# Cross-covariance attention: Q and K of a third of the heads in 8 KB rows

## The chip, the cores and the metric

The kernel runs on one core of a Trainium2 chip. A core has a matrix engine (TensorE, PE in the profile), three engines for elementwise work (VectorE or DVE, ScalarE or ACT, GpSimd or POOL), and SyncE (SP), which here issues all transfers between HBM and on-chip memory. Sixteen DMA engines move the bytes of each transfer side by side. Every engine works through its own instructions in order and waits for the others on semaphores. Matrix results go to PSUM, which GpSimd does not use here; everything else lies in SBUF, with 128 partitions.

The metric is the device time of one execution, in microseconds (us), as the median of several runs.

## The reference

There are 8 x 12 = 96 heads, with 512 positions n and 64 columns d each, all in float32. Attention is between columns, not positions:

```python
Q_norm = Q / (np.linalg.norm(Q, axis=-2, keepdims=True) + 1e-10)
K_norm = K / (np.linalg.norm(K, axis=-2, keepdims=True) + 1e-10)
attn = np.einsum('bhnd,bhne->bhde', Q_norm, K_norm)        # 64 x 64 per head
attn = np.exp(attn - np.max(attn, axis=-1, keepdims=True))
attn = attn / (np.sum(attn, axis=-1, keepdims=True) + 1e-10)
return np.einsum('bhnd,bhde->bhne', V, attn)
```

A norm is taken over the positions, so each head needs 64 norms of q, 64 of k and one 64 x 64 product (its gram). Q, K, V and the output are 12 MiB each: 36 MiB come in and 12 MiB go out.

## The kernel before

**Tiles.** A unit u is four heads (24 units), a pair s two units (12 pairs), a double pair w four units (6 of them, each with 1 MiB pieces of V).

**Loads.** `load_qk` (lines 170 to 180) brings Q and K of a pair as [128 partitions, 2 units, 16 positions, 64]. Each partition holds 16 neighbouring positions of one head, 4 KB of it, so 32 partitions (a row group of TensorE) hold one head. The last unit comes in 2 KB rows. `load_v` brings V with 32 positions to a partition, in 8 KB rows. There are three buffers for pairs of Q and K and three for V. Stores (`store`) write 512 KB in 2 KB rows from 13 buffers `so`.

**Grams.** `cast_qk` (line 196) casts a unit's Q and K on VectorE into one bf16 tile `qkb` with q and k side by side (two buffers). `grams` (208) multiplies each head's [q|k] with itself, 16 steps x 4 heads of 128 x 128 in four row groups. The result holds qq, qk, kq and kk. `squares` (222) picks the diagonals of qq and kk on VectorE (two instructions per pair, 64 partitions x 512), `sums` (237) reduces them to squared norms, `cross` (232) copies kq out of PSUM, `powers` (242) makes the reciprocal norms with a logarithm and an exponential on ScalarE.

**Attention.** `scale_k` (248) scales k's side on GpSimd or VectorE. `logits` transposes, `exps` scales by q's norm and exponentiates, `normalise` (271) divides and writes the bf16 tile `ab`. V is cast to bf16 (`cast_v`, on GpSimd or, late in the kernel, VectorE), transposed on TensorE (`vtrans`), copied out (`vcopy`) and multiplied with `ab` (`outs`); `ocopy` brings the result to `so`.

**Order.** All of this is written as pieces (`piece(key, engines, after, behind, rank, ...)`) with a guessed cost for each engine that may do it. `Order.run` plays them through and gives every engine a fixed order; nothing moves at run time. Keys: `cq` casts, `gr` grams, `sq` squares, `kq` cross, `rd` sums, `pw` powers, `sc` scale of k, `rq` scales of q, `lg` logits, `ex` exponentials, `nm` normalise, `cv` cast of v, `vt` transposes, `vc` their copies, `ou` outputs, `oc` their copies, `st` stores. From pair `BOTH` on, copies and casts may also go to VectorE (line 394, 409 ff., 430). All DMAs stand in one queue of SyncE in the planned order: a load that waits for a free buffer holds all loads and stores behind it.

Of the kernel before, what the change touches and what calls it, by code (L numbers as in the profile page):

```python
# [8 lines left out]
F32 = mybir.dt.float32  # L9
BF16 = mybir.dt.bfloat16  # L10
AF = mybir.ActivationFunctionType
# [91 lines left out]
def kernel(  # L103
# [13 lines left out]
    TAIL = 2  # L117
    WIDE = U - 1
    ONE = 3
    BOTH = S - 8  # L120
# [7 lines left out]
    Vu = V.rearrange("b h (p t) d -> (b h p) (t d)", t=2 * T).rearrange("(w r p) x -> w r p x", r=2, p=128)  # L128
# [9 lines left out]
    NB = dict(qk=3, v=3, vb=2, qkb=2, vt=2, so=13, sm=2, ab=4)  # L138
# [4 lines left out]
    qkp = ctx.enter_context(tc.tile_pool(name="qkp", bufs=NB["qkb"]))  # L143
    vtp = ctx.enter_context(tc.tile_pool(name="vtp", bufs=NB["vt"]))
# [5 lines left out]
    grams_only = ExitStack()  # L150
# [8 lines left out]

    qk32, v32, vb, qkb, gram, scr, kq, n2, r8, kqs, rq, lg, ex, ab, vps, vt, po, so = ({} for _ in range(18))  # L160
# [9 lines left out]
    def load_qk(s, x, r):  # L170

        w, e = divmod(s, 2)
        if s not in qk32:
            qk32[s] = qp.tile([128, 2, 2, T, D], F32, name="qk32")
        if 2 * s + (r or 0) >= WIDE:
            nc.sync.dma_start(out=qk32[s][:, x, r].rearrange("p (m j) d -> p m (j d)", m=2), in_=(Qw, Kw)[x][U - 1])
        elif r is None:
            nc.sync.dma_start(out=qk32[s][:, x].rearrange("p r t d -> p r (t d)"), in_=(Qu, Ku)[x][w, e])
        else:
            nc.sync.dma_start(out=qk32[s][:, x, r].rearrange("p t d -> p (t d)"), in_=(Qu, Ku)[x][w, e, :, r])  # L180
# [20 lines left out]

    def cast_v(eng, w, r, c):

        if w not in vb:
            vb[w] = vbp.tile([128, 2 * T, 2, D], BF16, name="vb")
        copy(eng, vb[w][:, c * T:(c + 1) * T, r], v32[w, r][:, c].rearrange("p (t d) -> p t d", d=D))

    def grams(u):


        s, r = divmod(u, 2)
        if r == 0:
            gram[s] = ps_g.tile([128, HU, 2, 2, 2 * D], F32, name="gram")
        for t in range(T if u < WIDE else J):
            for h in range(HU):
                if u < WIDE:
                    x = qkb[u][32 * h:32 * (h + 1), t, :]
                else:
                    x = qkb[u][64 * (h % 2):64 * (h % 2 + 1), J * (h // 2) + t, :]
                nc.tensor.matmul(gram[s][:, h, r, 0], x, x, start=(t == 0), stop=(t == (T if u < WIDE else J) - 1))  # L220

    def squares(s, n):

        if n == 0:
            scr[s] = small.tile([128, 2 * HU, D], F32, name="scr")
        half = (LO, HI)[n]
        nc.vector.scalar_tensor_tensor(  # L227
            out=scr[s][half], in0=gram[s][half, :, :, 0, half].rearrange("p h r d -> p (h r) d"), scalar=1e-20,
            in1=eye2[half, None, :].to_broadcast([D, 2 * HU, D]), op0=ALU.add, op1=ALU.mult,
        )  # L230

    def cross(eng, s):

        kq[s] = small.tile([128, 2 * HU, D], F32, name="kq")
        copy(eng, kq[s][HI], gram[s][HI, :, :, 0, LO].rearrange("p h r d -> p (h r) d"))

    def sums(s):
        n2[s] = small.tile([128, 2 * HU], F32, name="n2")
        nc.vector.tensor_reduce(out=n2[s], in_=scr[s], axis=mybir.AxisListType.X, op=ALU.add)  # L239

    def powers(s):

        ln = small.tile([128, 2 * HU], F32, name="ln")
        r8[s] = small.tile([128, 2 * HU], F32, name="r8")
# [3 lines left out]
    def scale_k(eng, s):  # L248
        kqs[s] = small.tile([128, 2 * HU, D], F32, name="kqs")
# [4 lines left out]
    def scales_q(s):  # L254

        rq[s] = small.tile([128, HU], F32, name="rq")
# [67 lines left out]

    abs_ = []
# [5 lines left out]
    def size(key):  # L331
        if key[0] == "gr" and key[1] >= WIDE:
            return 64
        return 8 if key[0] == "vt" and key[-1] is not None else {"gr": 128, "lg": 8, "vt": 16, "ou": 16}[key[0]]
# [3 lines left out]
    R = dict(cq=2.5, gr=2.471, sq=0.756, kq=1, rd=3.457, pw=3.5, sc=1, rq=1.9, lg=5, ex=1.1, nm=2.545, cv=1.165, vt=0.9, vc=1.1, ou=2, oc=0.9)  # L338
    BIAS = dict(sc=-0.6, kq=5, cv=1, vc=-0.3, oc=0.6)
    QK_PACE, V_FROM, V_PACE, ST_LAG = 0.631, 0.0377, 0.7486, 1.5133  # L340
# [4 lines left out]
    def piece(key, engines, after, behind, rank, fn, *args):  # L345
        if key[0] in ("cv", "vc", "oc", "kq", "sc"):
# [8 lines left out]
    def parts(s):  # L355
        return (0, 1) if s < ONE or s == S - 1 else (None,)

    def loaded(x, s, r):
        return ("l" + "qk"[x], s, r if len(parts(s)) == 2 else None)

    last = None
    for s in range(S):
        free = [back("cq", 2 * s + r, 2 * NB["qk"], x) for r in range(2) for x in range(2)]
        for r in parts(s):
            at = QK_PACE * (2 * s + (r or 0)) / U
            for x in range(2):
                key = loaded(x, s, r)
                piece(key, {"DMA": X if r is not None else 2 * X}, free, [last], at, load_qk, s, x, r)
                last = key
    for u in range(U):  # L370
        s, r = divmod(u, 2)
        piece(("cq", u, 0), {"DVE": 0.72}, [loaded(0, s, r), back("gr", u, NB["qkb"])], [back("cq", u, 1, 1)], R["cq"] + 0.01 * u, cast_qk, u, 0)
        piece(("cq", u, 1), {"DVE": 0.72}, [loaded(1, s, r)], [("cq", u, 0)], R["cq"] + 0.01 * u, cast_qk, u, 1)
        piece(("gr", u), {"PE": 1.6}, [("cq", u, 0), ("cq", u, 1), back("kq", s, 1)], [back("gr", u, 1)], R["gr"] + 0.01 * u, grams, u)
    for s in range(S):
        SM = NB["sm"]

        piece(("sq", s, 0), {"DVE": 0.70}, [("gr", 2 * s), ("gr", 2 * s + 1), back("rd", s, SM)], [], R["sq"] + 0.01 * s, squares, s, 0)
        piece(("sq", s, 1), {"DVE": 0.70}, [("gr", 2 * s), ("gr", 2 * s + 1)], [("sq", s, 0)], R["sq"] + 0.01 * s, squares, s, 1)
        piece(("kq", s), {"ACT": 0.60, "DVE": (0.70, BIAS["kq"])}, [("sq", s, 0), ("sq", s, 1), back("sc", s, SM)], [], R["kq"] + 0.01 * s, cross, s)  # L380
        piece(("rd", s), {"DVE": 0.69}, [("sq", s, 0), ("sq", s, 1), back("pw", s, SM)], [], R["rd"] + 0.01 * s, sums, s)
        piece(("pw", s), {"ACT": 0.5}, [("rd", s), back("rq", s, SM), back("sc", s, SM)], [], R["pw"] + 0.01 * s, powers, s)
        piece(("sc", s), {"POOL": (1.04, BIAS["sc"]), "DVE": 1.2}, [("pw", s), ("kq", s), back("lg", s, SM)], [], R["sc"] + 0.01 * s, scale_k, s)
        piece(("rq", s), {"ACT": 0.45}, [("pw", s), back("ex", s, SM)], [], R["rq"] + 0.01 * s, scales_q, s)
        piece(("lg", s), {"PE": 0.6}, [("sc", s), back("ex", s, 1)], [], R["lg"] + 0.01 * s, logits, s)
        piece(("ex", s), {"ACT": 1.30}, [("lg", s), ("rq", s), back("nm", s, NB["sm"])], [], R["ex"] + 0.01 * s, exps, s)
# [84 lines left out]
```

## Time and profile before

| | before |
|---|---|
| median of three runs | 130.85 us (130.26 to 130.95) |
| the profiled execution | 130.86 us |
| its span, first to last instruction | 129.1 us |
| last instruction of VectorE ends | 114.1 us |
| last copy to `so` ends (ScalarE) | 117.4 us |
| last store issued / landed | 119.3 / 128.1 us |
| bytes moved, mean rate | 50.64 MB, 392 GB/s |
| VectorE casts of Q and K (L200) | 48, mean 799 ns |
| VectorE squares (L227) | 24, mean 688 ns |
| GpSimd casts of V (L168) | 19, mean 1162 ns |
| GpSimd scale of k (L250) | 12, mean 1179 ns |

The profile is one execution. A group of its page gives the count, the busy time in us and the mean in ns. The slices cut the span into 40 parts of 3.2 us and give the busy share in tenths. The "landing" of a DMA is when its semaphore is complete.

### The profile page before, as it was taken

What the parts mean: (1) busy time and instruction counts of PE and PEld (TensorE: products, weight loads), DVE (VectorE), ACT (ScalarE), POOL (GpSimd) and SP (SyncE); (2) the same over time, 40 slices, a digit from 0 to 9 for tenths busy, and PEclk for the clock granted to TensorE, in tenths of its full rate; (3) what the DMA queues carried; (4) which work ended last, traced back from release to release, by engine and by line L of the source; (5) the groups of instructions that cost most, each with busy time, mean ns of one, the idle gap of its engine ahead of it and who ended that gap; (6) DMA issues with size and microseconds to landing.
All of it is one profiled execution on the core that took longest, in us unless ns stands there. A gap on an engine that the chain in (4) does not pass through costs nothing.

```text
span 129.1 us, 4881 instructions
## 1 busy us (share of the span) xinstructions
PE 77.8 (60%) x2128; PEld 63.3 (49%) x2128; DVE 91.0 (71%) x140; ACT 72.5 (56%) x220; POOL 37.3 (29%) x39
## 2 busy tenths in 40 slices
PE   0154384994837648967682986697785858382000
PEld 0144372773636537856572865486664746271000
DVE  3444649849999389699986798997999799830000
ACT  3000441569777085497783798383947969973000
POOL 3005406300813914043058003223463270300000
PEclk9999999999975685599999599655799999955555
DMA  4999999999999999999999999999999999999982
GB/s 133 389 430 410 432 399 409 408 416 409 422 406 411 404 408 410 402 413 430 410 414 406 416 415 418 405 420 415 405 410 403 405 399 406 402 407 406 408 312 75
DMA packets 15605, 50.64 MB, mean 392 GB/s; under 512 B 1120, under 2 KB 1632, under 8 KB 14176
## 3 DMA queue, kind: packets, MB, share of 16 engines
q1 hardware_dynamic: 15584, 50.34, 98.0%
q8 instruction: 16, 0.26, 0.8%
q14 instruction: 5, 0.04, 0.1%
HBM read 37.75 MB, written 12.58 MB: 390 GB/s over the span
## 4 chain that ended last, share of the span: by engine, by line
DMA 50%; DVE 16%; PE 10%; ACT 8%; issue 3%; SPq 1%; POOL 1%; ACTq 0%; POOLq 0%; DVEq 0%
DMA qk<-in_K_dram 21%; DMA v<-in_V_dram 15%; DMA qk<-in_Q_dram 14%; DVE qkb L200 7%; PE gram L220 6%; ACT so L164 3%; DVE scr L227 3%; DVE vt L166 2%; PE po L306 2%; DVE ab L278 2%; PE vps L289 2%; ACT ex L269 2%; ACT vt L164 2%; DVE n L239 1%; SPq L180 1%
## 5 line engine op out<-in xcount | busy, mean ns | idle before, releaser
L220 PE MATMUL gram<-qkb 32*128 32x128 bf16 (+1 forms) x1504 | 36.6, 259 | 21.7 <-DVE qkb L200 15.4
L200 DVE CAST qkb<-qk 128x1024 bf16<-128x1024 f32 x48 | 37.4, 799 | 11.7 <-DMA qk<-in_Q_dram 5.2
L220 PEld LDWEIGHTS <-qkb 32*128 32x128 bf16 (+1 forms) x1504 | 30.5, 116 | 26.8 <-DVE qkb L200 18.1
L168 POOL TENSOR_SCALAR vb<-v 128x1024 bf16<-128x1024 f32 x19 | 21.9, 1162 | 46.7 <-DMA v<-in_V_dram 46.4
L164 ACT COPY so<-po 128x512 f32<-128x512 f32 x45 | 25.0, 592 | 7.6 <-PE po L306 7.5
L164 ACT COPY vt<-vps 128x1024 bf16<-128x1024 bf16 (+1 forms) x18 | 17.8, 987 | 16.9 <-PE vps L289 16.8
L306 PE MATMUL po<-ab,vt 128*64 128x128 bf16 x384 | 21.3, 260 | 6.7 <-issue 2.8
L250 POOL TENSOR_TENSOR kqs<-kq,r 64x512 f32<-64x512 f32 x12 | 14.2, 1179 | 26.1 <-ACT r L246 14.1
L306 PEld LDWEIGHTS <-vt 128*64 128x64 bf16 x384 | 15.5, 131 | 10.8 <-issue 5.8
L289 PE MATMUL vps<-identb,vb 128*128 128x128 bf16 x192 | 16.7, 236 | 6.6 <-POOL vb L168 3.9
L227 DVE SCALAR_TENSOR_TENSOR scr<-gram,eye 64x512 f32<-64x512 f32 x24 | 16.5, 688 | 5.6 <-PE gram L220 5.3
L289 PEld LDWEIGHTS <-vb 128*128 128x128 bf16 x192 | 12.6, 105 | 9.6 <-POOL vb L168 4.9
L269 ACT ACTIVATE ex<-lg,rq 128x64 f32<-128x64 f32 x48 | 14.5, 322 | 2.8 <-PE lg L263 2.8
L164 ACT COPY kq<-gram 64x512 f32<-64x512 f32 x12 | 7.0, 581 | 14.4 <-DVE scr L227 14.0
L278 DVE TENSOR_TENSOR ab<-ex,rinv 64x256 bf16<-64x256 f32 x24 | 13.5, 560 | 0.6
L269 ACT ACTIVATION_READ_ACCUMULATOR ex<-lg,rq 128x1 f32 x48 | 10.2, 213 | 0.0
L263 PE MATMUL lg<-eye,kqs 64*128 64x64 f32 x48 | 6.6, 266 | 4.1 <-POOL kqs L250 2.8
L239 DVE TENSOR_REDUCE n<-scr 128x8 f32<-128x512 f32 x12 | 8.1, 678 | 0.1
L166 DVE COPY vt<-vps 128x1024 bf16<-128x1024 bf16 (+1 forms) x8 | 7.9, 1019 | 0.1
L263 PEld LDWEIGHTS lg<-eye,kqs 64*128 64x128 f32 x48 | 4.7, 162 | 6.0 <-POOL kqs L250 3.6
L166 DVE CAST vb<-v 128x1024 bf16<-128x1024 f32 x5 | 5.1, 1012 | 0.9 <-DMA v<-in_V_dram 0.9
L275 DVE RECIPROCAL rinv<-esum 128x4 f32<-128x4 f32 x12 | 2.1, 171 | 2.5 <-ACT ex L269 2.5
(15 smaller groups left out, 15.8 us busy)
## 6 DMA issues: line engine op xcount, KB each, us to landing
out_dram<-so SPq DMA_DIRECT2D x23, 512.0 KB, 10.2
v<-in_V_dram SPq DMA_DIRECT2D x11, 1024.0 KB, 17.9
qk<-in_Q_dram SPq DMA_DIRECT2D x8, 1024.0 KB, 18.2
qk<-in_K_dram SPq DMA_DIRECT2D x8, 1024.0 KB, 18.8
qk<-in_Q_dram SPq DMA_DIRECT2D x8, 512.0 KB, 12.1
qk<-in_K_dram SPq DMA_DIRECT2D x8, 512.0 KB, 12.5
v<-in_V_dram SPq DMA_DIRECT2D x2, 512.0 KB, 10.7
out_dram<-so SPq DMA_DIRECT2D x2, 256.0 KB, 9.1
```

Source lines behind the costliest of these rows:

```text
L164: nc.scalar.copy(o, i)
L166: nc.vector.tensor_copy(o, i)
L168: nc.gpsimd.tensor_scalar(out=o, in0=i, scalar1=1.0, scalar2=0.0, op0=ALU.mult, op1=ALU.add)
L200: nc.vector.tensor_copy(qkb[u][:, :, x * D:(x + 1) * D], qk32[s][:, x, r])
L220: nc.tensor.matmul(gram[s][:, h, r, 0], x, x, start=(t == 0), stop=(t == (T if u < WIDE else J) - 1))
L227: nc.vector.scalar_tensor_tensor(out=scr[s][half], in0=gram[s][half, :, :, 0, half].rearrange("p h r d -> p (h r) d"), scalar=1e-20, in1=e ...
L250: (nc.vector if eng == "DVE" else nc.gpsimd).tensor_tensor(out=kqs[s][HI], in0=kq[s][HI], in1=r8[s][HI, :, None].to_broadcast([D, 2 * HU, ...
L263: nc.tensor.transpose(l[:, h, :], kqs[s][HI, 2 * h:2 * h + 2].rearrange("p r d -> p (r d)"), eye2[HI])
L269: nc.scalar.activation(e[:, h, :], lg[s][:, h, :], AF.Exp, scale=rq[s][:, h:h + 1], accum_out=z[:, h:h + 1])
L278: nc.vector.tensor_tensor(out=a[half, :, half], in0=e[half], in1=ri[half, :, None].to_broadcast([D, HU, D]), op=ALU.mult,)
L289: nc.tensor.transpose(ps[:, c, n, :], vb[w][:, J * c + j].rearrange("p r d -> p (r d)"), identb)
L306: nc.tensor.matmul(po[s, x][e * D:(e + 1) * D, j].rearrange("p r d -> p (r d)"), v, ab[s][:, h, :])
```

## The change

For the double pairs w = 2 and 3 (pairs m = 4 to 7, 32 heads), Q and K come like V: 32 positions of a head in one partition, 8 KB rows, 1 MiB per transfer. Then 16 partitions hold a head, and a row group of 32 partitions holds two heads. To keep them apart, VectorE makes two copies of q in bf16, each with the other head's partitions multiplied by zero (`mask_q`), and the gram multiplies [q|k] of the row group with both masked q (64 matmuls of 128 columns per unit, as before). The result has qq and kq for both heads but no kk. k's squared norms are made another way: squares on ScalarE in f32 (`square_k`), halved five times by additions on GpSimd or VectorE (`fold_k`), and a matmul with a 0/1 matrix that adds each head's 16 partitions into a spare corner of the gram's PSUM (`norms_k`). Squares, copy, sums, powers and scaling are then done once for a double pair of 16 heads with 64 x 1024 elements, where two pairs had 64 x 512 (`big_squares` and so on). A double group holds the four banks of PSUM until `kQ`, `sQ` and `lK` are done; the next grams wait for these.

Four constants are added, `vb` gets a third buffer and `so` has 11 instead of 13, outputs may go to VectorE from pair 5 on (`BOTH`, 4 before), the last double pair is transposed in whole pieces, and the planner's ranks and paces are new, so the order of nearly all instructions is another. Bytes moved are the same, and so are the other 64 heads' steps.

```diff
-    TAIL = 2
+    TAIL = 4
...
-    BOTH = S - 8
+    BIG = (2, 3)
+    BOTH = S - 7
...
-    NB = dict(qk=3, v=3, vb=2, qkb=2, vt=2, so=13, sm=2, ab=4)
+    NB = dict(qk=3, v=3, vb=3, qkb=2, vt=2, so=11, sm=2, ab=4)
...
+        if big(m):
+            nc.sync.dma_start(out=qk32[m][:, x].rearrange("p c t d -> p (c t d)"), in_=(Qb, Kb)[x][w, e])
...
+    def mask_q(u):
+        mqb[u] = mqp.tile([128, T, 2, D], BF16, name="mqb")
+        for a in range(2):
+            nc.vector.tensor_scalar(
+                out=mqb[u][:, :, a], in0=qkb[u][:, :, :D], scalar1=half_of[:, a:a + 1], scalar2=None, op0=ALU.mult)
+
+    def square_k(u):
+        m, c = divmod(u, 2)
+        if c == 0:
+            ksq[m] = ksp.tile([128, 2, T, D], F32, name="ksq")
+        nc.scalar.activation(ksq[m][:, c], qk32[m][:, 1, c], AF.Square)
+
+    def fold_k(eng, m, part):
+        e = nc.vector if eng == "DVE" else nc.gpsimd
+        if part == 0:
+            e.tensor_tensor(out=ksq[m][:, 0], in0=ksq[m][:, 0], in1=ksq[m][:, 1], op=ALU.add)
+            return
+        ksum[m] = small.tile([128, D], F32, name="ksum")
+        n = T // 2
+        while n:
+            o = ksq[m][:, 0, :n] if n > 1 else ksum[m][:, None, :]
+            e.tensor_tensor(out=o, in0=ksq[m][:, 0, :n], in1=ksq[m][:, 0, n:2 * n], op=ALU.add)
+            n //= 2
...
+    def norms_k(m):
+        w, r = divmod(m, 2)
+        o = gram_of(w)[HI, 0, 4 * D:4 * D + 16].rearrange("p (h r) -> p h r", r=2)
+        nc.tensor.matmul(o[:, :, r], ksum[m], head_of, start=True, stop=True)
+
+    def big_grams(u):
+        m, c = divmod(u, 2)
+        w, r = divmod(m, 2)
+        g = gram_of(w)
+        for t in range(T):
+            for n in range(HU):
+                rows = slice(32 * n, 32 * (n + 1))
+                o = g[:, n, :4 * D].rearrange("p (a r d) -> p a r d", a=2, r=2)[:, :, r]
+                nc.tensor.matmul(o, qkb[u][rows, t], mqb[u][rows, t], start=(c == 0 and t == 0), stop=(c == 1 and t == T - 1))
...
+        if m >= NB["qk"] and big(m - NB["qk"]):
+            free += [("ks", 2 * (m - NB["qk"]) + i) for i in range(2)]
...
+        if big(m) and u % 4 == 0 or not big(m) and i == 0:
+            wait, release = release, [("kQ", w), ("sQ", w), ("lK", w)] if big(m) else [("kq", m)]
...
+            piece(("mq", u), {"DVE": 0.66}, [("cq", u, 0), back("gr", u, NB["qkb"])], [], R["mq"] + 0.01 * u, mask_q, u)
...
+            piece(("ks", u), {"ACT": 1.15}, [loaded(1, m, i)] + free, [back("ks", u, 1)] if i else [], R["ks"] + 0.01 * u, square_k, u)
...
+                    piece(("ka", m, n), {"POOL": 2.15, "DVE": (1.15, BIAS["ka"])}, [("ka", m, 0)] + [("kn", x) for x in older[:len(older) - 1]] if n else [("ks", u - 1), ("ks", u)], [],
+                          R["ka"] + 0.02 * m, fold_k, m, n)
+
+                piece(("kn", m), {"PE": 0.3}, [("ka", m, 1)], [("gr", 4 * w + 3)], R["kn"] + 0.02 * m, norms_k, m)
...
+        piece(("sQ", w), {"DVE": 1.2}, [("gr", 4 * w + k) for k in range(4)] + before(g, "rd", "sc"), [], R["sq"] + n, big_squares, w)
+        piece(("kQ", w), {"ACT": 1.15, "DVE": (1.2, BIAS["kq"])}, [("sQ", w)], [], R["kq"] + n, big_cross, w)
+        piece(("rD", w), {"DVE": 1.2}, [("sQ", w)] + before(g, "pw"), [], R["rd"] + n, big_sums, w)
...
+        piece(("lK", w), {"ACT": 0.25}, [("kn", 2 * w), ("kn", 2 * w + 1)] + free, [], R["lk"] + n, logs_k, w)
+        piece(("pW", w), {"ACT": 0.5}, [("rD", w), ("lK", w)] + before(g, "rq", "sc"), [], R["pw"] + n, big_powers, w)
+        piece(("sC", w), {"POOL": (2.1, BIAS["sc"]), "DVE": 1.25}, [("pW", w), ("kQ", w)] + before(g, "lg"), [], R["sc"] + n, big_scale_k, w)
+        piece(("rQ", w), {"ACT": 0.45}, [("pW", w)] + before(g, "ex"), [], R["rq"] + n, big_scales_q, w)
```

What the order becomes: VectorE gets 16 masks, two of the four first folds, both scalings of k, 12 output copies (3 before), 4 casts of v (5) and 4 copies of vt (5 and 3 half ones). GpSimd gets two first folds and all four fold tails, 20 casts of v (19) and 8 scalings of k (12). ScalarE gets 8 squares, 36 output copies (45) and 20 copies of vt (17 and a half one). SyncE issues as many transfers as before; 21 stores instead of 20 stand behind the last load of V.

## The prediction

> **What bounds the kernel now.** I read the page's busy shares and slices first, then the DMA rows, then the engines by stage, then single groups.
>
> ```profile
> PE 77.8 (60%) x2128; PEld 63.3 (49%) x2128; DVE 91.0 (71%) x140; ACT 72.5 (56%) x220; POOL 37.3 (29%) x39
> ...
> DMA  4999999999999999999999999999999999999982
> GB/s 133 389 430 410 432 399 409 408 416 409 422 406 411 404 408 410 402 413 430 410 414 406 416 415 418 405 420 415 405 410 403 405 399 406 402 407 406 408 312 75
> ...
> q1 hardware_dynamic: 15584, 50.34, 98.0%
> ```
>
> The transfers run from the second slice to the 38th without a hole: the kernel is bound by its DMA queue, and no engine is near full. The chain of waits agrees (DMA holds 50% of it). The landing records say how firmly: at every issue from the tenth on, exactly seven earlier transfers are still in flight. SyncE is held by the queue's depth, never by a missing buffer. The cover of a late issue is that backlog, 12 to 20 us of loads in the middle and about 10 us of stores at the end.
>
> The engines by stage (sums of busy us, in the order PE, PEld, DVE, ACT, POOL):
>
> ```profile
> 30.00:60.00 30.00, 20.86 (x644) 17.11 (x648) 25.82 (x40) 20.41 (x68) 11.44 (x10) 0.77 1.02 410
> 60.00:90.00 30.00, 22.09 (x616) 17.81 (x606) 25.68 (x39) 20.38 (x60) 9.38 (x8) 0.80 1.02 414
> 90.00:114.20 24.20, 16.88 (x426) 13.56 (x423) 22.03 (x35) 19.86 (x66) 8.96 (x8) 0.92 1.04 405
> ```
>
> From 30 us to its last instruction at 114.1, VectorE is busy 73.5 of 84.2 us, so only 10.7 us are free. It is the second resource to watch.
>
> Single instructions (duration min/median/max), and one meeting of VectorE and GpSimd in order of time (start, us):
>
> ```profile
> L200 DVE CAST qkb<-qk x48: 673/694/1534, 4.1 to 101.3; 128x1024 bf16<-128x1024 f32 x48
> ```
> ```profile
> L278 DVE TENSOR_TENSOR ab<-ex,rinv x24: 416/422/1167, 19.1 to 113.7; 64x256 bf16<-64x256 f32 x24
> ```
> ```profile
> 55.55 0.69 DVE L200 CAST qkb<-qk 128x1024 bf16<-128x1024 f32 x1
> ...
> 55.76 1.40 POOL L168 TENSOR_SCALAR vb<-v 128x1024 bf16<-128x1024 f32 x1 [4.51 <-DMA v<-in_V_dram]
> ...
> 56.16 1.53 DVE L166 CAST vb<-v 128x1024 bf16<-128x1024 f32 x1
> ```
>
> GpSimd's cast (1.05 us at the median) takes 1.40 behind VectorE's, and VectorE's next one (0.69 at the least) takes 1.53 behind GpSimd's. They take turns.
>
> **What the Trainium skill says.** "SBUF — State Buffer", section "Who interferes with whom": VectorE in a two-port mode, or with two SBUF inputs, and GpSimd hold one pair of ports exclusively; the second comer blocks. The lines above agree. The cost so far, mean less undisturbed duration: casts 48 x (799 - 694) = 5.0, ab 24 x (560 - 422) = 3.3, casts of v on VectorE 5 x (1012 - 686) = 1.6: 9.9 us of VectorE's 91. "DMA: Bandwidth & Descriptors", section "Why small descriptors are slow (HBM only)": a packet costs a few fixed cycles and a descriptor a fixed 32 bytes, so larger pieces gain a little. In the trace a 4 KB packet takes 159 ns at the median and an 8 KB one 312, not 318. Prices used below: "VectorE: DVE Perf Modes", section "Side-by-side: where the cycles go for N=2048 bf16", whose 4x mode gives an estimate of 0.42 us for 1024 elements (a quarter of them at 0.96 GHz, and the fixed part); no instruction of before shows it. "ScalarE: Activation LUTs", section "What ACT_TABLE_LOAD costs": 1024 elements take 1.0 to 1.1 us.
>
> **The change part by part.**
>
> *DMA.* Eight transfers of 1 MiB (Q and K of four pairs of units) go from 4 KB rows to 8 KB rows. V has these rows already: between landings V takes 2.45 to 2.51 us per MiB (mean 2.485), Q and K 2.50 to 2.57 (mean 2.545), late instruction fetches left out. Gain 8 x 0.06 = 0.48 us. By packets: 64 fewer pairs per DMA engine x (2 x 159 - 312) = 0.38 us. I take 0.45. Bytes, stores and the order at the start stay.
>
> *VectorE*, undisturbed, from the built order:
> - 16 mask instructions added (bf16, 128x1024): 0.42 each by the skill's price, 6.7 us. Bounds: 0.33 (4.8 in all, a little under the 4x price) to 0.69 (11.0, if they run as the f32 cast does).
> - Two folds of 1024 f32 pairs and two scalings of k with 1024 elements come to VectorE: 1.23 each, by the slope of the 512-element reduce (0.678) and squares (0.688): 4.9.
> - Squares: 8 x 0.688 become 2 x 1.22, -3.1. Sums: 4 x 0.678 become 2 x 1.22, -0.3.
> - Copies of the output: 3 become 12, +9 x 0.687 = 6.2. Copies of vt: 5 x 1.22 and 3 x 0.68 become 4 x 1.22, -3.3. Casts of v: 5 become 4, -0.7.
> - Two small reduces at the start, about 0.5, before data arrives: hidden.
> Sum after 30 us: +10.4.
>
> *GpSimd.* Casts 19 to 20, +1.0; scalings 12 to 8, -4.2; four fold tails of 512, 256, 128 and 64 pairs, 2.2 each by the 1.04 us that 512 pairs take at L250, +8.8; two full folds of 2.05, +4.1. Undisturbed 32.4 becomes 42.2.
>
> *Turns at the port.* Contending VectorE time was 48 x 0.694 + 24 x 0.422 + 5 x 0.686 = 46.9 us; now 46.9 - 0.7 + 6.7 + 4.9 = 57.8, x1.23. GpSimd x1.30. I scale the 9.9 us by both: 15.8, +5.9. Bounds: 0, if they never meet more often, and 12, if the fuller engine meets each time.
>
> *Sum on VectorE after 30 us*: 73.5 + 10.4 + 5.9 = 89.8 against 84.2 there were. It no longer fits; I keep half of the old idle time (5.4 of 10.7), because part of it is waiting on grams and on the last V, which lands about a store earlier. VectorE ends at 30 + 89.8 + 5.4 = 125.2, not 114.1.
>
> *What that may cost.* In the new order an output copy is VectorE's last work, with ScalarE's copies beside it; the last is then done some 1.2 us later, at 126.4 (two copies of 0.59). A quarter-MiB store in an empty queue needs about 2.7 us (the first load: 3.34 for half a MiB, of which 1.28 is transfer). It lands at 129.1, against 128.08 before: +1.0. Stores just ahead of it find the queue dry too and lose part of their backlog; I add 0.4. Against the profiled execution's 130.86 (span 129.1 and 1.8 around it; median of the runs 130.85) this is 132.2. The 0.45 of the DMA is then swallowed by waiting.
>
> *Hidden.* ScalarE: 8 squares x 1.1, -9 output copies x 0.59, +2.5 vt copies x 1.0: +6, into 56 us of idle. TensorE: the masked grams have the same 64 matmuls of 128 columns per unit, plus four small ones for the norms. If that cover is gone (TensorE throttled to half clock, as in slices 12 to 17), a gram of 1.9 instead of 1.07 us delays VectorE by its two-deep qkb; that is in the kept idle. SyncE: a load of pair m+3 now also waits for two ScalarE squares of pair m, and behind it stand V loads and stores; seven transfers are queued ahead of it, over 10 us of cover, so 2.2 us more are free. vb has three buffers instead of two and so 11 instead of 13: output n waits for store n-11 to land, 11 x 1.28 = 14 us ahead of its own; free.
>
> **The rivals.**
>
> *Still bound by DMA.* If VectorE ends before 125.3 - 1.2 = 124.1 us (128.08 less 2.7 for the store), nothing shows and the gain stays: 130.86 - 0.45 = 130.4, own range 130.0 to 131.2. For it: the queue never waited for data before; masks at 0.33 and fewer meetings at the port take 1.9 and several us off my sum. Against it: my sum passes the point by 1.1 us. This is the turning point; beyond it each us of VectorE is one of time.
>
> *Gram banks held.* A double group occupies all four gram banks until its k norms are read: K's landing, two squares (2.2), a fold (1.2 or 2.1), the tail (2.2), a small matmul and the logarithm, some 7 us in a row, before the next group's grams may start. Before, a copy of 0.58 behind two squares freed them. With qkb two deep the casts then stop. If VectorE loses 4 us in each of two groups, 8 instead of some 3 of the idle time that I kept, it ends 5 us later: 137. For it: TensorE's order puts the norm matmuls directly ahead of waiting work. Against it: TensorE is 60% busy and VectorE has masks of the next units to do meanwhile.
>
> *8 KB rows gain nothing*: then the first rival gives 130.8; V's cadence speaks against it.
>
> **How the numbers follow.** VectorE overfull 0.50, its own range 131.5 to 136.5 (the upper end with masks at 0.69, +4.3); gram banks 0.10; DMA still the bound 0.40. A measurement tells about 0.5% (0.65 us, the spread of the three runs). All of the first two is slower: 0.60. In the third 0.45 us is under the 0.65, so 0.24 within and 0.16 faster. The range from 130.0 to 137.0 leaves out about 0.1 on each side.
>
> **What would show it.** Right: VectorE at nine tenths in all slices from 30 us to the end, its last work near 125, masks near 0.42, longer means of L200 and L278, holes in the DMA row in the last eight slices, fewer than seven transfers in flight there, and Q and K of the middle pairs landing every 2.49 us. Wrong: seven in flight to the end and VectorE done before 124 (first rival); holes in the DMA row between 50 and 90 us (gram banks).

## The result and the profile after

The changed kernel takes 138.68 us (median of 4 runs, 138.42 to 139.58) against 130.9 for the kernel before in the same session: ratio 1.0607, 95% interval 1.0535 to 1.0678, so it is 6% slower. The forecast was 132.2, with a range of 130.0 to 137.0. The direction was right, the size was not, and the time lies outside the range. The profiled execution took 138.85 us, its span 137.0. Below, a time is the median of all runs of a kernel, while a ratio leaves out runs more than 1.5% above the kernel's fastest, so the two can differ (most in e16).

First the page of the changed kernel: busy shares, VectorE's and the DMA's row of the 40 slices, the rate, the queue.

```profile
PE 82.9 (61%) x2136; PEld 68.5 (50%) x2136; DVE 111.9 (82%) x158; ACT 77.0 (56%) x213; POOL 55.1 (40%) x56
...
DVE  4446679786699999997899999969899999799620
...
DMA  4999999999999999999999999999999992655895
GB/s 151 370 404 429 398 416 405 411 423 419 414 421 409 411 419 414 423 402 411 420 420 409 401 427 411 401 409 404 408 391 401 367 355 103 246 181 212 315 352 202
...
q1 hardware_dynamic: 14560, 50.34, 92.8%
```

The queue has no hole until slice 33, about 113 us, and is rarely full from there to the end. VectorE stands at nine tenths over most of the span. So the DMA isn't starved in the middle: the compute falls behind, uses up the backlog of loads, and the stores at the end are left waiting for it. SyncE's waits over the whole span (what the queue's issuer waited for, us in total, times, longest) say the same:

```profile
SPq L206 <- DVE so L173: 16.8, 7, 4.7
SPq L186 <- DVE qkb L212: 12.4, 3, 7.8
SPq L206 <- ACT so L171: 8.9, 10, 2.4
```

The stores wait for output copies, mostly VectorE's, and the loads for casts that free a buffer. In the kernel before, seven transfers stood in the queue at every issue from the tenth on; here there are as few as four at 73.5 us and none at 115.3. The chain that ended last has moved too:

```profile
DVE 44%; PE 29%; ACT 9%; DMA 7%; issue 5%; POOL 1%; SPq 1%; ACTq 0%; DVEq 0%; POOLq 0%
```

DMA held half of it before and holds 7% now. By stage (sums of busy us, PE, PEld, DVE, ACT, POOL, then clock, DMA share, GB/s), up to VectorE's last instruction, which ends at 131.6 (the last output copy, on ScalarE, ends at 132.9):

```profile
30.00:60.00 30.00, 17.75 (x516) 14.50 (x515) 27.07 (x33) 18.06 (x37) 17.86 (x17) 0.74 1.01 416
60.00:90.00 30.00, 20.92 (x500) 17.51 (x500) 27.60 (x34) 20.71 (x54) 17.27 (x15) 0.64 1.02 412
90.00:114.20 24.20, 17.16 (x465) 14.02 (x457) 22.98 (x34) 17.41 (x58) 8.64 (x7) 0.93 0.98 379
114.20:131.60 17.40, 13.27 (x256) 10.72 (x256) 14.35 (x25) 11.83 (x36) 2.52 (x2) 0.74 0.62 229
```

In the first two stages VectorE is busy 54.7 of 60 us (51.5 before) and GpSimd 35.1 (20.8 before); TensorE did fewer matmuls than before in the same time. Single instructions (duration min/median/max):

```profile
L212 DVE CAST qkb<-qk x48: 674/694/2126, 4.1 to 118.2; 128x1024 bf16<-128x1024 f32 x48
```
```profile
L218 DVE TENSOR_SCALAR mqb<-qkb,half_of x16: 467/506/2561, 36.8 to 74.9; 128x1024 bf16<-128x1024 bf16 x16
```
```profile
L376 DVE TENSOR_TENSOR ab<-ex,rinv x24: 417/422/1283, 21.0 to 129.4; 64x256 bf16<-64x256 f32 x24
```

The undisturbed durations stayed; the longest ones grew. A mask can take 2.56 us instead of 0.47. A stretch of the timeline (start, us, last column the idle time before it) shows why:

```profile
64.67 2.35 POOL L231 TENSOR_TENSOR ksq<-ksq 128x1024 f32<-128x1024 f32 x1 [2.95 <-ACT ksq L225]
65.43 3.81 DVE L212 CAST qkb<-qk 128x1024 bf16<-128x1024 f32 x2 [1.13 <-PE gram L260]
67.09 4.13 POOL L237 TENSOR_TENSOR ksq<-ksq 128x512 f32<-128x512 f32 x3
...
71.65 1.21 POOL L175 TENSOR_SCALAR vb<-v 128x1024 bf16<-128x1024 f32 x1
...
74.53 2.96 DVE L218 TENSOR_SCALAR mqb<-qkb,half_of 128x1024 bf16<-128x1024 bf16 x2
...
74.85 2.36 POOL L231 TENSOR_TENSOR ksq<-ksq 128x1024 f32<-128x1024 f32 x1 [1.98 <-ACT ksq L225]
```

Two casts take 3.81 us (1.39 undisturbed) while GpSimd folds; two masks take 2.96 (0.94 undisturbed) because the second comes just behind the start of a fold of 2.36 us and waits until that is over. The cast of V at 71.65 stood behind the folds; its data had landed at 62.88.

I split VectorE's time after 30 us in two: every instruction at the shortest duration that its form has in that trace (own work), and the rest (turns). Records of successive instructions overlap by 0.03 to 0.04 us on average, so these sums are 3 to 6 us above the busy time of the windows. Where a form has only two instances, both may have been held up, and the split is then rough; the sum is not.

| us after 30 us | own work | turns | sum | GpSimd busy |
|---|---|---|---|---|
| before | 66.2 | 10.4 | 76.6 | 29.9 |
| changed | 76.5 | 20.6 | 97.1 | 46.6 |

### The profile page after: what moved, and what is told of

It reads as the page before. It is cut to its first block, busy times and chain, and to the rows that moved or that the text cites. A ratio compares the mean times of both kernels' runs of the same rounds, so it can differ in the third digit from the quotient of the medians.

```text
span 137.0 us, 4930 instructions
## 1 busy us (share of the span) xinstructions
PE 82.9 (61%) x2136; PEld 68.5 (50%) x2136; DVE 111.9 (82%) x158; ACT 77.0 (56%) x213; POOL 55.1 (40%) x56
## 4 chain that ended last, share of the span: by engine, by line
DVE 44%; PE 29%; ACT 9%; DMA 7%; issue 5%; POOL 1%; SPq 1%; ACTq 0%; DVEq 0%; POOLq 0%
DVE qkb L212 17%; PE gram L317 15%; DVE mqb L218 8%; PE vps L387 6%; DMA qk<-in_K_dram 5%; DVE scr L325 5%; PE po L404 4%; ACT so L171 3%; DVE ab L376 2%; DVE ksq L231 2%; PE gram L260 2%; ACT vt L171 2%; DMA out_dram<-so 2%; ACT ex L367 2%; DVE vt L173 2%
## 5 line engine op out<-in xcount | busy, mean ns | idle before, releaser
L317 PE MATMUL gram<-qkb 32*128 32x128 bf16 (+1 forms) x992 | 24.8, 269 | 14.1 <-DVE qkb L212 10.4
L348 POOL TENSOR_TENSOR kqs<-scr,r 64x512 f32<-64x512 f32 x8 | 10.3, 1281 | 49.6 <-ACT r L344 21.5
L317 PEld LDWEIGHTS <-qkb 32*128 32x128 bf16 (+1 forms) x992 | 21.3, 121 | 16.6 <-DVE qkb L212 11.8
L171 ACT COPY vt<-vps 128x1024 bf16<-128x1024 bf16 x20 | 20.2, 1010 | 13.6 <-PE vps L387 13.4
L404 PEld LDWEIGHTS <-vt 128*64 128x64 bf16 x384 | 16.0, 132 | 10.5 <-issue 7.6
L260 PE MATMUL gram<-mqb,qkb 32*128 32x128 bf16 x512 | 12.0, 263 | 9.3 <-DVE mqb L218 6.9
L260 PEld LDWEIGHTS <-qkb 32*128 32x128 bf16 x512 | 10.8, 118 | 10.3 <-issue 7.6
L237 POOL TENSOR_TENSOR ksq<-ksq 128x512 f32<-128x512 f32 (+2 forms) x12 | 12.5, 1042 | 5.2 <-DVE ksq L231 4.4
L225 ACT ACTIVATE ksq<-qk 128x1024 f32<-128x1024 f32 x8 | 8.2, 1058 | 8.0 <-POOL ksum L237 7.9
L218 DVE TENSOR_SCALAR mqb<-qkb,half_of 128x1024 bf16<-128x1024 bf16 x16 | 11.7, 771 | 0.1
L173 DVE COPY so<-po 128x512 f32<-128x512 f32 x12 | 7.9, 686 | 3.5 <-PE po L404 3.4
```

Of the source, the lines that this page charges most:

```text
L171: nc.scalar.copy(o, i)
L218: nc.vector.tensor_scalar(out=mqb[u][:, :, a], in0=qkb[u][:, :, :D], scalar1=half_of[:, a:a + 1], scalar2=None, op0=ALU.mult)
L237: e.tensor_tensor(out=o, in0=ksq[m][:, 0, :n], in1=ksq[m][:, 0, n:2 * n], op=ALU.add)
L260: nc.tensor.matmul(o, qkb[u][rows, t], mqb[u][rows, t], start=(c == 0 and t == 0), stop=(c == 1 and t == T - 1))
L404: nc.tensor.matmul(po[s, x][e * D:(e + 1) * D, j].rearrange("p r d -> p (r d)"), v, ab[s][:, h, :])
```

## The experiments

Five theories went into them. The *VectorE theory* (V) is the prediction's: its own work and its turns with GpSimd no longer fit. The *gram theory* (G) is the second rival: the banks are held until the norms of k are read. The *order theory* (O): the new ranks, paces and buffers cost by themselves. The *buffer theory* (K): the single buffer of the squares chains ScalarE to GpSimd. The *GpSimd theory* (P): GpSimd with its folds is too full and too slow beside VectorE. Each comparison has its own runs of the kernel before (130.4 to 131.1 us), and ratios are to these.

### Rows and order

**e1**, the rows alone, in the kernel before:

```diff
...
+        elif w in (2, 3):
+            nc.sync.dma_start(out=qk32[s][:, x].rearrange("p r t d -> p (r t d)"), in_=(Qb, Kb)[x][w, e])
```

> The kernel before, with one thing changed: Q and K of pairs 4 to 7 come in 8 KB rows. The arithmetic behind them stays as it was, so those 32 heads are computed on wrongly arranged data; every instruction and its order are those of before. It measures the DMA's part of the change alone. Theory V (VectorE overfull, the rows themselves gain): 0.45 us less, 130.4, a ratio near 0.9965, with the 1 MiB transfers of these pairs landing every 2.49 us instead of 2.545. Theory R (8 KB rows of Q and K gain nothing or cost): 130.8 to 131.5.

Measured: 130.12 us, ratio 0.9950 (0.9931 to 0.9969). The rows are worth 0.65 us in the order and with the buffers of before.

**e4**, the changed kernel with no pair of units in the new form:

```diff
-    BIG = (2, 3)
+    BIG = ()
```

> The changed kernel with no head in the new form (BIG empty): 4 KB rows and the old arithmetic for all heads, but with the new buffers (vb 3, so 11), BOTH and TAIL, ranks and paces. It computes all of the reference. Theory V: 130.6 to 131.5, bound by DMA as before. Theory O (the new order and the smaller so are what costs): 133 or more.

Measured: 132.04, ratio 1.0110 (1.0074 to 1.0146). The new order and buffers cost about 1% before any mask or fold.

**e11**, the same with the buffers of before:

```diff
-    NB = dict(qk=3, v=3, vb=3, qkb=2, vt=2, so=11, sm=2, ab=4)
+    NB = dict(qk=3, v=3, vb=2, qkb=2, vt=2, so=13, sm=2, ab=4)
```

> The changed kernel without 8 KB rows, masks, squares and folds, as in the run that took 132.0, but with 2 buffers of vb and 13 of so as before the change; only the ranks and paces that set the order are new. If the 1% of that run came from the buffers: 130.6 to 131.0. If it came from the order: 131.7 to 132.4.

Measured: 131.5, ratio 1.0052 (1.0030 to 1.0073), between the two expectations. It was not compared with e4 on the same chip, and e15 below shows no gain from the same buffers, so how the 1% divides between order and buffers stays open.

### Folds

**e3**, no squares and no folds:

```diff
-        nc.scalar.activation(ksq[m][:, c], qk32[m][:, 1, c], AF.Square)
+        return
...
-        e = nc.vector if eng == "DVE" else nc.gpsimd
...
+        ksum[m] = fixed
```

> The changed kernel without the squares of k (ScalarE) and without the folds (GpSimd and VectorE); the norm matmuls read a constant tile, so the k norms of 32 heads are constant. Masks and order stay. Theory V: VectorE loses 3.3 us of folds and most of the 12 us that its waiting for GpSimd grew by; the time falls to 130.5 to 132.5. If VectorE's own work alone counts and the turns at the port do not: 135 to 136. Theory G: the chain to the norms shrinks too, 130.5 to 133.

Measured: 131.42, ratio 1.0056 (1.0036 to 1.0077). Nearly the whole loss goes with them, though the 16 masks stay. V and G had both forecast this; it doesn't tell them apart. VectorE's sum after 30 us is 86.3 (own 74.1, turns 12.2).

**e7**, the folds as 32 accumulating matmuls on TensorE:

```diff
-    ksp = ctx.enter_context(tc.tile_pool(name="ksp", bufs=1))
+    ksp = ctx.enter_context(tc.tile_pool(name="ksp", bufs=2))
...
-            ksq[m] = ksp.tile([128, 2, T, D], F32, name="ksq")
+            ksq[m] = ksp.tile([128, 2, T, D], BF16, name="ksq")
...
-        nc.tensor.matmul(o[:, :, r], ksum[m], head_of, start=True, stop=True)
+        for n in range(2 * T):
+            nc.tensor.matmul(o[:, :, r], ksq[m][:, n // T, n % T], head_of, start=(n == 0), stop=(n == 2 * T - 1))
```

> The changed kernel with the squares of k written as bf16 into two buffers, and the fold and sum over partitions done by TensorE: 32 small matmuls per pair that add up in PSUM in place of one. No fold on GpSimd or VectorE; all of the reference is computed. TensorE gets 4 x 31 more small matmuls, about 4 x 4 us. Theories K and P: 130.5 to 132.5, as in the run without folds (131.4). Theory G: the matmuls lengthen the hold of the banks by some 3 us per double pair: 133 to 136.

Measured: 130.54, ratio 0.9999 (0.9979 to 1.0018): all of the work done (the squares rounded to bf16), and level with the kernel before. Own 74.0, turns 11.9. So with the masks in place it is the folds on VectorE and GpSimd that cost, not the squares, the norms or the masked grams.

**e8**, all folds on VectorE:

```diff
-        e = nc.vector if eng == "DVE" else nc.gpsimd
+        e = nc.vector
```

> The changed kernel with all folds on VectorE; GpSimd has none. VectorE gets about 9 us more of its own work (four tails of 1.6 us, two first folds of 1.2) and loses the waits for GpSimd's folds, some 8 us; GpSimd loses about 17 us. Theory K: the serial chain shrinks from 9.6 to about 6 us per pair, the time falls to 132 to 135. Theory P: 132 to 134. Theory V (VectorE's sum decides): no better than the changed kernel, 138 or more.

Measured: 138.77, ratio 1.0587 (1.0496 to 1.0678): no gain. Turns fell to 12.8 us, but own work rose to 85.3, the sum to 98.1. The windows of this run, 60 to 90 us:

```profile
60.00:90.00 30.00, 20.64 (x500) 17.82 (x501) 28.91 (x47) 20.38 (x53) 3.27 (x3) 0.60 1.02 412
```

VectorE has 1.1 us left and GpSimd is idle: own work alone overfills it.

### Masks

**e2**, no masks:

```diff
-        mqb[u] = mqp.tile([128, T, 2, D], BF16, name="mqb")
-        for a in range(2):
...
+        return
...
-                nc.tensor.matmul(o, qkb[u][rows, t], mqb[u][rows, t], ...
+                nc.tensor.matmul(o, qkb[u][rows, t], qkb[u][rows, t, None, :D].to_broadcast([32, 2, D]), ...
```

> The changed kernel without its 16 mask instructions; the grams read unmasked q twice instead, so the two heads of a row group are mixed. Same order of everything else. Theory V: VectorE loses 11.7 us of busy time (16 x 0.771), of which about 8 stood on the path, so the time falls from 138.7 to 130.4 to 132. Theory G (the gram banks held for the k norms set the pace): the masks are not in that chain, and the time stays at 136 to 138.5.

Measured: 137.44, ratio 1.0472 (1.0412 to 1.0532). This went against the VectorE theory: 12 us fewer on VectorE (sum 84.7) and only 1.2 us gained. The waits between 30 and 90 us name what took over:

```profile
ACT ksq L222 <- POOL ksum L234: 7.8, 2, 4.3
...
PEld gram L246 <- POOL ksum L234: 6.3, 2, 5.7
PE gram L246 <- POOL ksum L234: 6.1, 2, 5.6
```

TensorE stands some 6 us (the last two lines are its loader and its matmuls, one stretch twice) in front of the norm matmuls until GpSimd's tails are done, with the next work queued behind them. The kernel is still 6.7 us above the kernel before.

**e9**, no masks and the folds on VectorE (e2 and e8 together):

> Two edits at once: the masks are taken out (the grams of the eight double units read q unmasked, so their logits mix two heads) and all folds of the squares go to VectorE. Joint room of VectorE and GpSimd (either edit alone leaves one of the two too full: without masks GpSimd's folds hold the chain, with the folds on VectorE that engine has no idle time): together they leave VectorE about 27 of each 30 us and GpSimd about 3, no turns at the port, so 131 to 133 us. Length of the chain (K's squares, fold, norm, next grams, however the engines are loaded): the folds stay in the chain, so no better than without masks alone, 136 to 138.

Measured: 131.18, ratio 1.0048 (1.0020 to 1.0076). Alone the edits gained 1.2 us and nothing, together 7.5. Its own work on VectorE, 77.9 us, is more than the changed kernel's 76.5; its turns are 11.8 instead of 20.6. But the wait for GpSimd's tails is gone too, so e9 alone doesn't tell turns from waits; e13 and e17 below do.

### Links: what waits for the folds

**e5**, two buffers of squares (paid with two of so):

```diff
-    ksp = ctx.enter_context(tc.tile_pool(name="ksp", bufs=1))
+    ksp = ctx.enter_context(tc.tile_pool(name="ksp", bufs=2))
...
-    sop = ctx.enter_context(tc.tile_pool(name="sop", bufs=NB["so"]))
+    sop = ctx.enter_context(tc.tile_pool(name="sop", bufs=9))
```

> The changed kernel with two buffers for the squares of k instead of one; to make room, 9 buffers for outputs instead of 11. Every engine's order is the same and all of the reference is computed. Theory K (a new one, after the run without folds: the squares of the next pair wait on ScalarE until the fold tail of the last pair has freed the only ksq tile, so square, fold and tail run one after the other, once in about 9.6 us, and ScalarE's queue stands behind them): the 7.9 us wait of the squares for ksum goes and the time falls to 131 to 134. Theory G (gram banks held for the k norms): 136 to 138.7. Theory P (GpSimd is too full and too slow beside VectorE): 135 to 138.7.

Measured: 138.7, ratio 1.0628 (1.0557 to 1.0700). ScalarE's wait of 7.9 us for ksum is gone and the time stayed, which speaks against the buffer theory. That the two output buffers given up cost as much as was gained is not ruled out by this run.

**e6**, norms of k not read:

```diff
-        nc.tensor.matmul(o[:, :, r], ksum[m], head_of, start=True, stop=True)
+        return
...
-        nc.scalar.activation(lnk[w][HI], gram["w", w][HI, 0, 4 * D:4 * D + 16], AF.Ln, bias=tiny[HI])
+        nc.scalar.activation(lnk[w][HI], fixed[HI], AF.Ln, bias=tiny[HI])
```

> The changed kernel without the norm matmuls and with the logarithm of the k norms taken from a constant; squares and folds still run, their result is not used, so 32 heads have a constant k norm. The gram banks then come free after squares and copy alone. Theory G: the time falls to 131 to 133. Theory K: 136 to 138.7, the wait of the squares for ksum stays near 8 us. Theory P: 136 to 138.7.

Measured: 136.83, ratio 1.0487 (1.0425 to 1.0549). The gram theory is worth at most about 1.9 us of the 8; e13 below cuts the same link and gains nothing.

**e13**, folds that nobody waits for:

```diff
...
-        e = nc.vector if eng == "DVE" else nc.gpsimd
+        e, z = (nc.vector, zd) if eng == "DVE" else (nc.gpsimd, zp)
...
-            e.tensor_tensor(out=o, in0=ksq[m][:, 0, :n], in1=ksq[m][:, 0, n:2 * n], op=ALU.add)
+            e.tensor_tensor(out=z[:, :n], in0=z[:, :n], in1=z[:, n:2 * n], op=ALU.add)
...
```

> The folds run in the same places of the order and in the same sizes, but on a tile of zeros of their own: they wait for nothing and nobody waits for them. The squares are still computed and read by nobody, the norm matmuls are left out, the logarithm of k's norms reads a constant; so k is not normalised. Masks are kept. If the folds cost by the time that they hold GpSimd and the port: 135.5 to 137, as with the norms unread (136.8). If they cost by the waits for their inputs and results: 131 to 132.5.

Measured: 138.68, ratio 1.0589 (1.0531 to 1.0646). No link through squares, folds and norms is left, and the loss is whole (even a little above the expected 137): with the masks in place the folds cost by their time. In the profile (of the run that took 139.8) VectorE's sum is 98.1 (own 78.3, turns 19.8). Both of its folds met GpSimd and took 2.05 us instead of 1.21, so 1.7 us of that own work are turns. Beside e7, which has masks and squares too, the turns grew by 9.6 us and the own work by 2.6: the greater part is turns.

**e14**, no masks and norms unread (e2 and e6 together):

> Masks taken out (grams of the double units read q unmasked, two heads mixed) and the norms of k not read (no norm matmuls, the logarithm reads a constant); the folds stay on GpSimd behind the squares. Alone, the first edit gained 1.2 us and the second 1.9. If what is left is GpSimd's time and the V casts queued behind its folds: 134.5 to 136. If the wait for the norms and VectorE's masks are two causes of which either alone is enough: 131 to 132.5.

Measured: 137.65 in the median, but its runs go from 134.29 to 137.94, so no ratio is given. The edit left the folds behind the squares and V's casts behind the folds. In its profile (137.93 us, waits between 30 and 90 us) TensorE's loader waits longest for those casts:

```profile
PEld L384 <- POOL vb L175: 14.1, 5, 5.8
```

So casts of V behind the folds can hold the kernel up though no norm is read; but with one run at 134.29, how the wait of e2 divides is not settled.

**e17**, no masks and unlinked folds (e2 and e13 together):

> The folds unlinked as in the run that took 138.7 (on zeros of their own, nobody waits for them, k is not normalised), and the masks taken out too (grams of the double units read q unmasked, two heads mixed). If without masks the loss of the linked kernel (137.4) came from waits for the folds and their inputs: 131 to 132.5. If GpSimd's time on the folds alone, with V's casts queued behind them, is enough: 136 to 138.

Measured: 131.4, ratio 1.0033 (1.0010 to 1.0056). So without masks it is the links that hold the kernel at 137.4, and with masks (e13) it is the time. Either is enough alone, which is why taking away one of them showed so little. VectorE's sum is 88.5.

### The cause put into the kernel before

**e18**, the kernel before with its own order, rows and buffers, and the time of masks and folds added, read by nobody:

```diff
+        if s in (4, 5, 6, 7) and x == 0:
+            for a in range(2):
+                nc.vector.tensor_scalar(out=spare[:, :, a], in0=qkb[u][:, :, :D], scalar1=ones[:, a:a + 1], scalar2=None, op0=ALU.mult)
+        if s in (4, 5, 6, 7) and x == 1 and r == 1:
+            e, z = (nc.vector, zd) if s < 6 else (nc.gpsimd, zp)
+            e.tensor_tensor(out=z, in0=z, in1=z, op=ALU.add)
+            n = T // 2
+            while n:
+                nc.gpsimd.tensor_tensor(out=zp[:, :n], in0=zp[:, :n], in1=zp[:, n:2 * n], op=ALU.add)
+                n //= 2
...
```

> The kernel before, in its own order, rows and buffers, all of it computed, with the time of the masks and folds added and nothing else: 16 masks of ones on VectorE into a tile that nobody reads, 2 folds of 1024 pairs on VectorE, 2 on GpSimd, and 4 tails on GpSimd, on zeros. If the room of the two engines and their port is the cause: about 12 us more of port work on VectorE and 19 on GpSimd, between 39 and 70 us, where 29 of 100 were free: 135 to 140. If the loss needs the new order or the links of norms and grams: 131 to 132.5.

Measured: 139.21, ratio 1.0612 (1.0559 to 1.0665), as much as the change lost, without its links, its order or its grams. Its windows:

```profile
30.00:60.00 30.00, 14.97 (x416) 12.29 (x416) 29.14 (x36) 15.75 (x51) 21.13 (x19) 0.66 1.02 411
60.00:90.00 30.00, 20.21 (x476) 16.85 (x477) 29.46 (x40) 14.18 (x40) 14.72 (x14) 0.66 0.89 354
```

and its waits between 30 and 90 us:

```profile
PEld L231 <- DVE qkb L200: 18.9, 6, 4.7
PE gram L231 <- DVE qkb L200: 18.6, 7, 4.5
```

VectorE has 1.4 us free of 60, and TensorE waits for its casts for some 19 us. Own work is 76.7 (+10.5), turns 22.1 (+11.7). The time of masks and folds is enough for the loss. The way it reaches the end differs in one point: here the queue runs short from 60 to 90 us already (354 GB/s), in the changed kernel after 113.

The sums beside the times (of the kernels in which own work or turns were the question):

| kernel | own work | turns | sum | time, us |
|---|---|---|---|---|
| e3 no folds | 74.1 | 12.2 | 86.3 | 131.4 |
| e7 folds on TensorE | 74.0 | 11.9 | 85.9 | 130.5 |
| e17 no masks, unlinked | 69.3 | 19.2 | 88.5 | 131.4 |
| e9 no masks, folds on VectorE | 77.9 | 11.8 | 89.7 | 131.2 |
| e6 norms unread | 75.9 | 20.6 | 96.4 | 136.8 |
| changed | 76.5 | 20.6 | 97.1 | 138.7 |
| e8 folds on VectorE | 85.3 | 12.8 | 98.1 | 138.8 |
| e13 unlinked | 78.3 | 19.8 | 98.1 | 138.7 |
| e18 load in the kernel before | 76.7 | 22.1 | 98.7 | 139.2 |
| e2 no masks | 68.4 | 16.4 | 84.7 | 137.4 |

Up to 89.7 us the time stays within 131.5; from 96.4 on it is above 136.5, and no run lies between. Of these only e2 falls out, and e17 shows that links hold it. A small sum alone promises nothing: e14 (85.4) and, below, e10 (89.8) and e12 (75.3) have long times, with VectorE idle for 18 to 30 us after 30 us. What goes with the time in all profiles is when VectorE's last instruction ends: at 123.8 us or before in every kernel that took up to 132.0 us, at 129.0 or later in all that took 136.8 or more (e16 between, at 124.8).

### Other engines, and a faster version

**e10**, V's casts from GpSimd to ScalarE:

```diff
-        copy(eng, vb[w][:, c * T:(c + 1) * T, r], ...
+        copy("ACT" if eng == "POOL" else eng, vb[w][:, c * T:(c + 1) * T, r], ...
```

> The casts of V that GpSimd does go to ScalarE, in the same places of the order; folds and scalings stay on GpSimd. Nothing is left out. Queue theory (V waits on GpSimd behind folds, so TensorE's transposes and the outputs come late, and each meeting at the port costs VectorE): V no longer waits, GpSimd's busy time falls from 55 to about 33 us, 132 to 135 us. Chain theory (the wait is for folds and norms before the next grams, V only follows): 137 to 139.

Measured: 140.32, ratio 1.0750 (1.0705 to 1.0796), outside both expectations. VectorE's turns fell to 13.1 and its sum to 89.8, yet the time rose: ScalarE is busy 24.6 and 24.1 of each 30 us between 30 and 90 (18.1 and 20.7 in the changed kernel), and its queue also holds exponentials and output copies for the other engines. That this is what cost the time is read from the busy times and not tested.

**e12**, folds on TensorE (e7) and the masks on ScalarE:

```diff
-            nc.vector.tensor_scalar(out=mqb[u][:, :, a], in0=qkb[u][:, :, :D], scalar1=half_of[:, a:a + 1], ...
+            nc.scalar.activation(mqb[u][:, :, a], qkb[u][:, :, :D], AF.Copy, scale=half_of[:, a:a + 1])
```

> Folds as accumulating matmuls on TensorE (the run that took 130.5) and, besides, the masks on ScalarE instead of VectorE (16 x about 1.05 us). Nothing is left out. If VectorE's end (125.0 us in that run) still set the time, VectorE loses 11 us and the queue alone is left, with the gain of the rows: 129.8 to 130.3. If the masks on ScalarE come late behind its exponentials and copies and hold the grams: 131 to 133.

Measured: 139.08, ratio 1.0618 (1.0582 to 1.0653), worse than both expectations. The windows of this run:

```profile
30.00:60.00 30.00, 19.11 (x546) 16.63 (x544) 18.32 (x22) 26.25 (x42) 11.51 (x10) 0.74 1.01 421
60.00:90.00 30.00, 21.65 (x533) 19.60 (x535) 17.07 (x25) 26.56 (x59) 3.81 (x3) 0.63 1.02 405
```

VectorE is idle 40% of the time, and ScalarE takes its place with 26.4 of 30 us: 16 masks of 1.15 us in a queue that also holds exponentials, squares and copies. The second expectation had this path, with too small a cost; it too is read from the busy times.

**e15**, e7 with the buffers of before (vb 2, so 13), and **e16**, besides that the ranks and paces of before:

> Folds as matmuls on TensorE with all else computed (130.5 before), and 2 buffers of vb and 13 of so as before the change. Nothing is left out. If the buffers' 0.5% returns: 129.8 to 130.2. If the queue is already full without it: 130.3 to 130.7.

> As the run before it, and the order of the work planned with the ranks and paces of the kernel before and with costs that fit the folds on TensorE. Nothing is left out. If the order's 0.5% returns: 129.6 to 130.2, faster than both kernels. If ranks made for the other pieces fit these badly: 131 to 134.

Measured: e15 130.85, ratio 1.0025 (1.0004 to 1.0046); e16 135.83, ratio 1.0322 (1.0267 to 1.0376). Neither is faster than e7, and no version here that computes the reference beats the kernel before. The rows alone were worth 0.65 us (e1), and e7 loses that again; whether to the order or to its late last copy (125.0) was not tried.

## Why the prediction was right or wrong

- **The bound before, and the turning point.** Right. It named VectorE as the next bound, with a turning point at 124.1 us for VectorE's end: kernels in which it ended at 123.8 or before took at most 132.0 us, and those with 129.0 or later lost 6 us or more.
- **Gain of the rows**, 0.45: e1 measured 0.65. Q and K of the middle pairs landed 2.49 us apart, as said. Nothing of it was left in the changed kernel's time.
- **VectorE's own work**, +10.4: measured 76.5 - 66.2 = +10.3. Masks 7.5 instead of 6.7 (shortest 0.467, while the estimate from the Trainium skill, "VectorE: DVE Perf Modes", section "Side-by-side: where the cycles go for N=2048 bf16", was 0.42), folds and scalings 4.9 (4.9), output copies +6.1 (6.2), copies of vt -3.3 (-3.3).
- **GpSimd's own work.** Tails were put at 2.2 each; undisturbed they took 3.0: 1.33, 0.78, 0.52 and 0.38 us for 512, 256, 128 and 64 pairs. Two full folds took 4.7 (4.1). The folds thus hold GpSimd for 16.7 us at their shortest, not 12.9.
- **Turns**, +5.9: measured +10.2, inside the stated bounds of 0 to 12. This term was mis-sized. It was scaled from a kernel whose GpSimd pieces are of 1 us; a fold can hold VectorE up for nearly as long as it lasts, up to 2.1 us at once. The Trainium skill, "SBUF — State Buffer", section "Who interferes with whom", says that the one that comes second blocks for the whole instruction, and the trace agrees (a mask of 0.467 us took 2.56 beside a fold of 2.36). Own work and turns together grew by 20.5, of which 2 are a larger overlap of the records: in busy time VectorE came to 92.0 us, where 89.8 had been forecast.
- **"I keep half of the old idle time (5.4 of 10.7)".** This step failed. VectorE's last instruction ended at 131.6 us, not at 125.2: 30 + 92.0 busy + 9.6 idle, where the working had 30 + 89.8 + 5.4. Of the 6.4 us, 4.2 are idle time and 2.2 the mis-sized turns. Nearly all of the old idle time stayed. Up to 114.2 us it was 6.6, near the assumption; the other 3.0 came in the 17.4 us after that, which the working had as all busy. There VectorE's output copies waited for TensorE (VectorE's waits, 114.2 to 131.6 us):

```profile
DVE so L173 <- PE po L404: 2.8, 3, 1.2
```

How much idle time stays is no constant: e18 kept 4.7 us, near the assumption, and reached its time with 94.4 us of busy VectorE. What sets it was not tried.
- **The end** held: the last copy 1.3 us after VectorE (1.2 forecast), and from there to the last landing 3.1 (132.9 to 136.0), where 2.7 and 0.4 for a dry queue had been said.
- **The signs.** Holes in the DMA row and fewer than seven transfers in flight at the end, longer means of the casts (895 ns, 799 before) and of ab (611, 560 before): they came. VectorE's last work came at 131.6, not near 125, and the masks took 0.77 us on average, not 0.42.
- **Hidden work.** ScalarE and TensorE: right as far as e3 and e7 show. SyncE's cover held (no hole before 113 us), though from 33 us on the seven in flight fell at times to 4 to 6. The new buffers and order were taken as free: e4 shows 1%.
- **Rival 2, gram banks held**, gave 137, the nearest number, but that is luck: its sign, holes in the DMA row between 50 and 90 us, did not come, and the loss stays without its link (1.9 us gained in e6, nothing in e13). Yet waits for the folds are a second cause that is enough by itself: without masks they hold the kernel at 137.4 (e2 beside e17). **Rival 1** fell with the turns and the idle time: VectorE ended 7.5 us behind its turning point.
- **The range** ended at 137.0 because the dear ends (turns of 12, all idle time kept) were not taken together: 30 + 73.5 + 10.4 + 12 + 10.7 puts VectorE's end at 136.6 and the time at 143.6 by the prediction's own steps. One slip is in the working: 16 masks of 0.33 us are 5.3 us, not 4.8, so that bound takes 1.4 off the sum, not 1.9. No number of the forecast rests on it.

What stays open: how the 1% of e4 divides; what part of e2's wait is the norms and what part V's casts (e14); why e13, which cuts more than e6, was not faster than it; and the clock. TensorE's granted clock between 60 and 90 us was 0.60 to 0.72 in the kernels that lost 6 us or more and 0.78 to 0.90 in those that didn't, e16 (0.67) between. Which follows from which wasn't tried. In e18 it can't be the whole cause: after 30 us VectorE had 4.7 us of idle time, 1.4 of it before 90, and a faster TensorE can't save it more waiting than that, of a loss of 8 us. Within one kernel the time doesn't go with the mean clock (two runs of e7 with a mean of 0.79 and 0.89: 130.1 and 130.4 us).

## What to carry to other kernels

Count VectorE and GpSimd as a pair: give each long GpSimd instruction its own price in VectorE's waiting, up to its full length each time they meet, and give a stage that is prolonged its own idle time, since its waits for other engines stay. When taking one suspect away gains little, take two away together before giving the theory up: here masks and links each held the time alone. And work moved to an engine with 40% idle time isn't free when that engine's queue feeds the others: with the masks on ScalarE (e12) the kernel took 139.1 us, as long as the changed one.

## What the runs showed of the hardware

- A VectorE instruction that meets a GpSimd one can wait for nearly all of it: a mask of 0.467 us took 2.56 beside a fold of 2.36.
- Not every VectorE instruction waits. After 30 us in the changed kernel the squares and copies read from PSUM ran 6.5 us beside GpSimd instructions and the f32 sums in SBUF 2.0 us; their turns are 0.2 and 0.1 us. Casts of Q and K, masks, and the products that make ab ran 32.9 us beside them and had 18.1 of the 20.6.
- Small GpSimd folds cost more than in proportion to their size: at the least 1.33 us for 512 pairs, 0.78 for 256, 0.52 for 128 and 0.38 for 64. And 512 f32 sums on 128 partitions (1.33) cost more than 512 products on 64 partitions (1.04), from which the prediction had priced them.
- The same mask of 1024 bf16 elements took 0.467 us on VectorE and 1.13 at the least on ScalarE.
